# A row softmax on one core: from pooled 4-row tiles to one in-place arena with tiles of up to 16 rows and hand-placed semaphores

## The chip, the cores and the metric

The kernel runs on one core of a Trainium2 chip. The metric is the device time of one execution in microseconds (us), lower is better. Six kinds of unit matter here: the 16 DMA engines that move data between HBM and SBUF; VectorE (DVE); ScalarE (ACT), which also issues DMAs; SyncE (SP), which here only issues DMAs and waits; GpSimd (POOL), which is idle (0.2 us busy); and each engine's sequencer (ACTq, SPq). All runs compared below are fast runs of one core at clock 1.000 unless I say otherwise.

A ratio below is the mean time of one kernel's fast runs over the mean of the other kernel's fast runs of the same rounds. It is therefore not quite the ratio of the medians that I quote beside it.

## The reference

```python
# x: float32 (16, 1024, 512), so 16384 rows of 512
x_scaled = x / 2.0
x_max = np.max(x_scaled, axis=-1, keepdims=True)
exp_x = np.exp(x_scaled - x_max)
return exp_x / np.sum(exp_x, axis=-1, keepdims=True)
```

Every partition of SBUF gets 128 rows of 2 KB. 33.55 MB are read and 33.55 MB are written. Nothing is reused.

## The kernel before

A tile is 128 partitions by 4 rows (1 MB), so each partition's part of a DMA is one run of 8 KB. There are 32 tiles. Loads are issued by SP, stores by ACT, and a framework places the semaphores and may reorder the instructions of an engine.

```python
R = 4
in_pool  = ctx.enter_context(tc.tile_pool(name="inp",  bufs=8))
out_pool = ctx.enter_context(tc.tile_pool(name="outp", bufs=8))
...
def do_load(i):
    x_sb = in_pool.tile([P, R, D], fp32, name=f"x_sb")
    nc.sync.dma_start(out=x_sb, in_=xt[i])
    nc.vector.reduce_max(out=negmax, in_=x_sb, axis=mybir.AxisListType.X, negate=True)
def do_exp(i):                      # ACT, one instruction per row, plus row sums
    for r in range(R):
        nc.scalar.activation(out=e_sb[:, r], in_=x_sb[:, r], func=Exp,
            bias=negmax[:, r:r+1], scale=0.5, accum_out=sums[:, r:r+1])
    nc.vector.reciprocal(out=recip, in_=sums)
def do_mul(i):                      # DVE, one instruction per row
    ...
def do_store(i):
    nc.scalar.dma_start(out=ot[i], in_=e_sb)
for j in range(TOT):                # load j, exp j-1, multiply j-2, store j-3
    ...
```

The softmax here doesn't subtract the row's maximum and nothing guards it: scores larger than these inputs give would overflow.

Of the kernel before, what the change touches and what calls it, by code (L numbers as in the profile page):

```python
# [1 line left out]

# [4 lines left out]


@with_exitstack  # L10
def kernel(
    ctx: ExitStack,
    tc: tile.TileContext,
    x: bass.AP,
    out: bass.AP,
):
    nc = tc.nc
    fp32 = mybir.dt.float32

    xf = x.flatten_outer_dims()  # L20
    of = out.flatten_outer_dims()
    N, D = xf.shape
    P = nc.NUM_PARTITIONS

    R = 4
    rows_per_tile = P * R
    ntiles = N // rows_per_tile

    xt = xf.rearrange("(n p r) d -> n p r d", p=P, r=R)
    ot = of.rearrange("(n p r) d -> n p r d", p=P, r=R)  # L30

    in_pool = ctx.enter_context(tc.tile_pool(name="inp", bufs=8))
    out_pool = ctx.enter_context(tc.tile_pool(name="outp", bufs=8))
    st_pool = ctx.enter_context(tc.tile_pool(name="stats", bufs=8))

    LAG_EXP = 1
    LAG_MUL = 2
    LAG_ST = 3
    TOT = ntiles + LAG_ST

    x_sbs = {}
    e_sbs = {}
    negmaxs = {}
    sumss = {}
    recips = {}

    def do_load(i):
        x_sb = in_pool.tile([P, R, D], fp32, name=f"x_sb")
        nc.sync.dma_start(out=x_sb, in_=xt[i])  # L49
        negmax = st_pool.tile([P, R], fp32, name=f"negmax")  # L50
        nc.vector.reduce_max(  # L51
            out=negmax, in_=x_sb, axis=mybir.AxisListType.X, negate=True
        )
        x_sbs[i] = x_sb
        negmaxs[i] = negmax

    def do_exp(i):
        x_sb = x_sbs.pop(i)
        negmax = negmaxs[i]
        e_sb = out_pool.tile([P, R, D], fp32, name=f"e_sb")  # L60
        sums = st_pool.tile([P, R], fp32, name=f"sums")
        for r in range(R):
            nc.scalar.activation(  # L63
                out=e_sb[:, r],
                in_=x_sb[:, r],
                func=mybir.ActivationFunctionType.Exp,
                bias=negmax[:, r : r + 1],
                scale=0.5,
                accum_out=sums[:, r : r + 1],
            )  # L70
        recip = st_pool.tile([P, R], fp32, name=f"recip")
        nc.vector.reciprocal(out=recip, in_=sums)  # L72
        e_sbs[i] = e_sb
        recips[i] = recip

    def do_mul(i):
        e_sb = e_sbs[i]
        recip = recips[i]
        for r in range(R):
            nc.vector.tensor_scalar_mul(  # L80
                out=e_sb[:, r],
                in0=e_sb[:, r],
                scalar1=recip[:, r : r + 1],
            )

    def do_store(i):
        e_sb = e_sbs.pop(i)
        nc.scalar.dma_start(out=ot[i], in_=e_sb)  # L88

    for j in range(TOT):  # L90
        if j < ntiles:
            do_load(j)
        if 0 <= j - LAG_EXP < ntiles:
            do_exp(j - LAG_EXP)
        if 0 <= j - LAG_MUL < ntiles:
            do_mul(j - LAG_MUL)
        if 0 <= j - LAG_ST < ntiles:
            do_store(j - LAG_ST)


# [1 line left out]
_INS = ['x']  # L102
_OUTS = [((16, 1024, 512), 'float32')]


# [23 lines left out]
```

## Time and profile before

| | before |
|---|---|
| time | 165.8 us |
| span in the profile | 163.8 us |
| bytes moved | 67.15 MB |
| DVE busy, ACT busy | 78%, 58% |
| steady DMA rate, 24 to 136 us | 427 GB/s |

The first block holds lines of the page. The slices cut the span into 40 equal pieces, and each digit is the busy share in tenths. The GB/s row and the windows book a packet, with all of its bytes and time, where it starts, so a share can come out over 1.00. In the groups, the columns after the bar are busy time, mean ns of one instruction, and the idle time before them with its main releaser.

```profile
span 163.8 us, 663 instructions
DVE 128.3 (78%) x192; ACT 94.4 (58%) x257; POOL 0.2 (0%) x4
DVE  0599999585699689998977778978778977977540
ACT  0399777706052625776676545676555676599900
DMA  4999999999999999999999999999999999799995
GB/s 174 436 422 422 348 422 432 426 424 428 426 426 428 422 426 432 424 428 426 426 432 428 424 430 424 428 426 426 428 428 424 426 430 424 326 414 412 418 420 228
q1 hardware_dynamic: 4608, 33.56, 49.2%
q10 hardware_dynamic: 4608, 33.56, 48.7%
DMA 63%; ACT 13%; DVE 9%; issue 7%; ACTq 2%; SPq 2%; DVEq 0%
L63 ACT ACTIVATE e_sb<-x_sb,negmax 128x512 f32<-128x512 f32 x128 | 90.7, 709 | 55.6 <-DVE e_sb L80 50.5
L51 DVE TENSOR_REDUCE negmax<-x_sb 128x4 f32<-128x2048 f32 x32 | 73.0, 2282 | 24.8 <-DMA x_sb<-in_x_dram 24.8
L80 DVE TENSOR_SCALAR e_sb<-e_sb,recip 128x512 f32<-128x512 f32 x128 | 53.5, 480 | 0.9
```

The DMA row reads 9 nearly everywhere, so I take the DMA engines for the limit, and the 55.6 us of idle ACT cost nothing by themselves. Two slices stand out in the GB/s row: 348 near the start and 326 near the end. Each queue has 4608 packets: 4096 of data (32 tiles x 128 partitions, 8 KB each) and 512 semaphore writes.

The windows view puts sizes on the two dips. Its columns are the stretch, its length, busy time and count of DVE, ACT and POOL, the clock, the DMA share, and GB/s.

```profile
16.00:20.00 4.00, 4.00 (x7) 3.41 (x10) 0.00 (x0) 1.00 1.00 338
24.00:136.00 112.00, 93.46 (x131) 61.52 (x168) 0.00 (x0) 1.00 1.01 427
140.00:144.00 4.00, 3.93 (x12) 2.56 (x7) 0.00 (x0) 1.00 0.76 311
144.00:160.00 16.00, 9.74 (x27) 11.65 (x34) 0.00 (x0) 1.00 1.01 418
```

The two dips differ in kind. At 16 us the engines are fully busy (share 1.00) but slower: the load packets that start from 16 to 20 us took 395 ns on average instead of 309 from 24 to 136 us. At 140 us they are idle for a quarter of the time (share 0.76): the loads have ended and the next stores are not ready. I call that one the hole.

### The profile page before, as it was taken

What the parts mean: (1) busy time and instruction counts of PE and PEld (TensorE: products, weight loads), DVE (VectorE), ACT (ScalarE), POOL (GpSimd) and SP (SyncE); (2) the same over time, 40 slices, a digit from 0 to 9 for tenths busy, and PEclk for the clock granted to TensorE, in tenths of its full rate; (3) what the DMA queues carried; (4) which work ended last, traced back from release to release, by engine and by line L of the source; (5) the groups of instructions that cost most, each with busy time, mean ns of one, the idle gap of its engine ahead of it and who ended that gap; (6) DMA issues with size and microseconds to landing.
All of it is one profiled execution on the core that took longest, in us unless ns stands there. A gap on an engine that the chain in (4) does not pass through costs nothing.

```text
span 163.8 us, 663 instructions
## 1 busy us (share of the span) xinstructions
DVE 128.3 (78%) x192; ACT 94.4 (58%) x257; POOL 0.2 (0%) x4
## 2 busy tenths in 40 slices
DVE  0599999585699689998977778978778977977540
ACT  0399777706052625776676545676555676599900
POOL 0000000000000000000000000000000000000000
DMA  4999999999999999999999999999999999799995
GB/s 174 436 422 422 348 422 432 426 424 428 426 426 428 422 426 432 424 428 426 426 432 428 424 430 424 428 426 426 428 428 424 426 430 424 326 414 412 418 420 228
DMA packets 9221, 67.15 MB, mean 410 GB/s; under 512 B 1024, under 2 KB 1024, under 8 KB 1024
## 3 DMA queue, kind: packets, MB, share of 16 engines
q1 hardware_dynamic: 4608, 33.56, 49.2%
q10 hardware_dynamic: 4608, 33.56, 48.7%
q14 instruction: 5, 0.04, 0.1%
HBM read 33.55 MB, written 33.55 MB: 410 GB/s over the span
## 4 chain that ended last, share of the span: by engine, by line
DMA 63%; ACT 13%; DVE 9%; issue 7%; ACTq 2%; SPq 2%; DVEq 0%
DMA x_sb<-in_x_dram 63%; ACT e_sb L63 13%; DVE e_sb L80 6%; DVE negmax L51 3%; ACTq L88 2%; SPq L49 2%; DVE recip L72 1%; DVEq L124 0%; ACTq L63 0%
## 5 line engine op out<-in xcount | busy, mean ns | idle before, releaser
L63 ACT ACTIVATE e_sb<-x_sb,negmax 128x512 f32<-128x512 f32 x128 | 90.7, 709 | 55.6 <-DVE e_sb L80 50.5
L51 DVE TENSOR_REDUCE negmax<-x_sb 128x4 f32<-128x2048 f32 x32 | 73.0, 2282 | 24.8 <-DMA x_sb<-in_x_dram 24.8
L80 DVE TENSOR_SCALAR e_sb<-e_sb,recip 128x512 f32<-128x512 f32 x128 | 53.5, 480 | 0.9
L63 ACT ACTIVATION_READ_ACCUMULATOR e_sb<-x_sb,negmax 128x1 f32 x128 | 23.9, 187 | 0.0
L72 DVE RECIPROCAL recip<-sums 128x4 f32<-128x4 f32 x32 | 5.4, 169 | 3.7 <-ACT e_sb L63 3.7
L63 ACT ACT_TABLE_LOAD x1 | 1.3, 1283 | 5.6 <-DMA x_sb<-in_x_dram 5.6
L113 POOL MEMSET const-uint8-127<- 128x1 uint8 x1 | 0.1, 102 | 0.0
L113 POOL MEMSET const-bfloat16-1.0<- 128x1 bf16 x1 | 0.1, 101 | 0.0
L113 POOL MEMSET const-float32-0.0<- 128x1 f32 x1 | 0.1, 99 | 0.2 <-issue 0.2
L113 POOL MEMSET const-float32-1.0<- 128x1 f32 x1 | 0.1, 98 | 0.0
## 6 DMA issues: line engine op xcount, KB each, us to landing
x_sb<-in_x_dram SPq DMA_DIRECT2D x32, 1024.0 KB, 12.2
out_dram<-e_sb ACTq DMA_DIRECT2D x32, 1024.0 KB, 10.0
```

Source lines behind the costliest of these rows:

```text
L49: nc.sync.dma_start(out=x_sb, in_=xt[i])
L51: nc.vector.reduce_max(out=negmax, in_=x_sb, axis=mybir.AxisListType.X, negate=True)
L63: nc.scalar.activation(out=e_sb[:, r], in_=x_sb[:, r], func=mybir.ActivationFunctionType.Exp, bias=negmax[:, r : r + 1], scale=0.5, accum_ ...
L72: nc.vector.reciprocal(out=recip, in_=sums)
L80: nc.vector.tensor_scalar_mul(out=e_sb[:, r], in0=e_sb[:, r], scalar1=recip[:, r : r + 1],)
L88: nc.scalar.dma_start(out=ot[i], in_=e_sb)
L113: nc = _bacc.Bacc("TRN2", target_bir_lowering=False, num_devices=1)
```

## The change

The intent is to keep DMA busy from end to end. One tensor ("arena") of 100 rows per partition holds everything and each row is computed in place. Tiles grow to 16 rows, so a partition's run is up to 32 KB. Eight loads (100 rows) are issued at once on ACT's queue. The last 28 rows reuse the places of early tiles, and their loads are issued on SP between the stores. All waits are placed by hand.

```diff
+PLAN = [                      # (rows, place in the arena)
+    (4, 0), (8, 4), (16, 12), (16, 28), (16, 44), (16, 60), (16, 76),
+    (8, 92), (16, 12), (8, 4), (4, 0),
+]
+ARENA = 100
+CHUNK = 4
+LAG = 2
...
-    R = 4
-    in_pool = ctx.enter_context(tc.tile_pool(name="inp", bufs=8))
-    out_pool = ctx.enter_context(tc.tile_pool(name="outp", bufs=8))
+    arena = nc.alloc_sbuf_tensor("arena", (P, ARENA, D), fp32)
...
+    def dram(ap, t):
+        b, r, _ = tiles[t]
+        return ap[b * P : (b + r) * P].rearrange("(p r) d -> p r d", r=r)
...
+    with tc.tile_critical():
+        for t in range(len(tiles)):
+            if t not in behind:          # behind: tiles whose place it reuses
+                nc.scalar.dma_start(out=sb(t), in_=dram(xf, t)).then_inc(ld[t], 16)
+        for k, (t, b, a) in enumerate(chunks):
+            ...  # ACT: exp of 4 rows in place, waits s_max, then s_exp
+        for k in range(len(chunks) + LAG):
+            ...  # DVE: max of chunk k (waits ld), multiply of chunk k-2 (waits s_exp)
+        late = sorted(behind)
+        for t in range(len(tiles)):
+            nc.sync.wait_ge(s_mul, last_chunk[t] + 1)
+            nc.sync.dma_start(out=dram(of, t), in_=sb(t)).then_inc(st[t], 16)
+            while late and max(behind[late[0]]) <= t - 2:
+                u = late.pop(0)
+                for v in behind[u]:
+                    nc.sync.wait_ge(st[v], 16)
+                nc.sync.dma_start(out=sb(u), in_=dram(xf, u)).then_inc(ld[u], 16)
+        for t in range(len(tiles)):
+            nc.sync.wait_ge(st[t], 16)
```

## The prediction

> **What bounds the kernel now.** The DMA engines: the page's slices show them 90% or more busy from slice 2 to the end; DVE is 78% busy, ACT 58%. The windows view gives a steady 427 to 428 GB/s (24 to 136 us), at which 67.15 MB take 157 us of the 163.8 us span. The other 6 to 7 us, from the windows view: 2.4 us before bytes flow, 0.8 us in a dip to 311-319 GB/s at 17 to 20 us when stores begin, 1.1 us at 140 to 142 us (DMA share 0.70 and 0.39: loads have ended, stores are not ready), 0.5 us because the stores-only end runs at about 418 GB/s, and 1.7 us after the last bytes. The large idle sums in the waits view (ACT 55.6 us, DVE 24.8 us) cost nothing by themselves.

> **What the change does.** Bytes and compute stay the same (reduction 2.29 us per 4 rows, exp 0.71 us and multiply 0.42 us a row, reciprocal 0.17 us). In one arena, 100 of 128 rows per partition are requested at once; the last 28 reuse early rows.

> 1. The 140 us hole closes. DVE needs about 4.2 us per 4-row chunk. I estimate that it waits for the third tile until about 21 us, then runs without a break to about 147 us. Loads end near 120 to 125 us with two tiles or more of finished stores queued; the last stores become ready about 137, 145 and 147 us, ahead of the DMA. Gain 1.1 us, all critical.
> 2. Fewer, longer descriptors: 22 DMAs in place of 64, runs of 32 KB for 96 of 128 rows in place of 8 KB. Fewer semaphore writes (9 ns each, 64 down to 22 per engine): 0.4 us. At the steady rate an 8 KB packet costs about 305.5 ns[...]. [...]
> 3. Swapping queues does nothing to bandwidth; it frees ACT of 0.34 us per store, off the critical path. Late loads travel on SP's queue before the stores of tile 5; they do not starve the DMA.
> 4. Against it: the stores-only end grows from about 20 to 37 us at 2% less bandwidth, minus 0.4 us. Start-up and tail are unchanged.

> **Sum.** 165.8 - 1.1 - 0.4 - 0.7 + 0.4 - 0.7 (a softer dip) = 163.3 us. Range 161.6 to 165.0. Faster by over 2%: 0.30; within 2%: 0.66; slower by over 2%: 0.04.

> **What would show it.** Right: no slice below 90% DMA between slice 2 and the last; no hole near 140 us; steady rate 428 to 433 GB/s; DVE almost continuously busy from about 21 to 147 us and done over 8 us before the end; a chain of waits dominated by DMA. The packet count shows whether long runs stay whole (about 2,800 data packets in place of 8,192). Wrong: a hole before the last stores, DVE stalled on loads after 21 us, or 8 KB packets as before.

> **What would make it wrong.** [...] long packets slowing one direction or leaving engines uneven at the end; stores held behind the late loads so that DMA idles; a slower start with ACT issuing.

The sum came to 163.3 us. The first "- 0.7" in it is half of an estimate for the longer runs that rested on figures no trace or run shows. Without it the sum would be 164.0 us. Two more things rest on such figures: the upper end of the steady rate, 433 GB/s, and a case under what would make it wrong.

## The result and the profile after

The changed kernel takes 164.37 us (median of four fast runs, 163.9 to 164.8) against 165.76 us. The ratio is 0.9912, with a 95% interval of 0.989 to 0.9933. A second set on another occasion gave 164.5 us and 0.9916. The change gains 0.9%, which is within 2%.

These are the answering lines of the page after:

```profile
span 162.7 us, 528 instructions
DVE 127.0 (78%) x192; ACT 95.0 (58%) x257; POOL 0.2 (0%) x4
DVE  0539199999999999999976999997999999920000
ACT  0378547777777777777770777775777777600000
DMA  4999998989999999999999999999999999999992
GB/s 161 427 443 508 395 419 379 486 371 411 447 449 395 475 427 403 475 411 395 443 451 419 407 435 425 443 435 387 389 457 435 419 451 389 435 483 403 411 413 103
q1 hardware_dynamic: 2016, 40.90, 59.0%
q10 hardware_dynamic: 1152, 26.21, 38.1%
DVE 53%; DMA 33%; issue 1%; ACTq 1%; SPq 0%
L99 DVE TENSOR_REDUCE negmax<-arena 128x4 f32<-128x2048 f32 x32 | 72.9, 2280 | 15.3 <-DMA arena<-in_x_dram 15.3
```

The computing is the same and from 20 us on it runs with two short breaks; it ends at 143.4 us, and the last four DVE slices are 0. The queues hold 2016 + 1152 = 3168 packets: 2816 of data and 352 semaphore writes, so the 32 KB runs travel whole. The GB/s row scatters more mostly because a long packet is booked into the slice where it starts: spread over their durations, the packets give 430 GB/s and a share of 1.00 for 16 to 20 us, where the windows view below says 508 and 1.21. In the chain, DVE has replaced DMA as the largest share. That looks like a new limit, and experiment 3 tests it.

The same windows after:

```profile
16.00:20.00 4.00, 0.89 (x3) 2.68 (x8) 0.00 (x0) 1.00 1.21 508
24.00:136.00 112.00, 107.49 (x165) 79.71 (x219) 0.00 (x0) 1.00 1.01 428
140.00:144.00 4.00, 3.39 (x9) 1.01 (x4) 0.00 (x0) 1.00 1.13 483
144.00:160.00 16.00, 0.00 (x0) 0.00 (x0) 0.00 (x0) 1.00 0.93 400
```

The hole at 140 us is gone. The steady rate is 428 GB/s against 427. The last line is low because packets that started before 144 us are booked earlier and because most engines have finished before 160 us. Spread over their durations, the packets run at 432 GB/s from 144 to 158 us, against 418 in the kernel before.

The trace records every packet with its start and duration. For each DMA it holds 16 semaphore writes (352 for 22 DMAs, 1024 for 64); I take those of the last store for one from each engine when its part has landed. From these I made a ledger. "Bulk ends" is the median of those 16 last writes.

| us | before | after | difference |
|---|---|---|---|
| bulk of the engines ends at | 161.91 | 159.59 | -2.32 |
| the last engine after the bulk | 0.69 | 1.36 | +0.67 |
| last semaphore to the end of the span | 1.16 | 1.71 | +0.55 |
| span | 163.75 | 162.67 | -1.09 |

Within the -2.32 us: the first byte comes at 1.92 instead of 1.75 us (+0.17), the hole had cost 0.99 us per engine (-0.99), packets above their usual duration (the median for their size) took 2.14 us per engine more than usual instead of 1.68 (+0.46), and the rest, about -2.0 us, I put down to the longer packets and the fewer semaphore writes. Their usual durations in the trace are 309 ns (8 KB), 611 ns (16 KB) and 1213 ns (32 KB). Where a single engine is left alone in a trace (the tail of experiment 9), the starts of its packets follow each other every 306 ns and 607 ns, so a packet costs about 301 ns per 8 KB plus 5 ns each. For the plan of the changed kernel that is 96 x 1209 + 48 x 607 + 32 x 306 ns = 155.0 us per engine, where the 1209 ns are extrapolated, against 512 x 306 ns = 156.7 us before: 1.7 us less. Forty-two fewer semaphore writes per engine add an estimated 0.2 us, at about 5 ns each: their records take 9 ns, of which I take off the 3 to 4 ns by which a packet overlaps the next (309 against 306 ns, 611 against 607).

So the gain was there, about 2.3 us, and half of it was given back in the last three microseconds. These are single executions; the second traced execution of the changed kernel (experiment 11) has nearly the same end.

### The profile page after: what moved, and what is told of

Read it like the earlier page. It is cut to its first block, busy times and chain, and to the rows that moved or that the text cites. A ratio compares the mean times of both kernels' runs of the same rounds, so it can differ in the third digit from the quotient of the medians.

```text
span 162.7 us, 528 instructions
## 1 busy us (share of the span) xinstructions
DVE 127.0 (78%) x192; ACT 95.0 (58%) x257; POOL 0.2 (0%) x4
## 3 DMA queue, kind: packets, MB, share of 16 engines
q1 hardware_dynamic: 2016, 40.90, 59.0%
q10 hardware_dynamic: 1152, 26.21, 38.1%
## 4 chain that ended last, share of the span: by engine, by line
DVE 53%; DMA 33%; issue 1%; ACTq 1%; SPq 0%
DMA arena<-in_x_dram 33%; DVE negmax L99 28%; DVE arena L112 24%; DVE recip L108 1%; ACTq L81 1%; SPq L131 0%; ACTq L164 0%; SPq L70 0%
## 5 line engine op out<-in xcount | busy, mean ns | idle before, releaser
L84 ACT ACTIVATE arena<-arena,negmax 128x512 f32<-128x512 f32 x128 | 90.8, 710 | 40.9 <-DVE negmax L99 40.9
L99 DVE TENSOR_REDUCE negmax<-arena 128x4 f32<-128x2048 f32 x32 | 72.9, 2280 | 15.3 <-DMA arena<-in_x_dram 15.3
L112 DVE TENSOR_SCALAR arena<-arena,recip 128x512 f32<-128x512 f32 x128 | 53.6, 482 | 1.1
L84 ACT ACTIVATION_READ_ACCUMULATOR arena<-arena,negmax 128x1 f32 x128 | 23.9, 187 | 0.0
```

Source lines behind the costliest of these rows:

```text
L84: ins = nc.scalar.activation(out=arena[:, a + r], in_=arena[:, a + r], func=mybir.ActivationFunctionType.Exp, bias=negmax[:, b + r : b + r ...
L99: nc.vector.reduce_max(out=negmax[:, b : b + CHUNK], in_=arena[:, a : a + CHUNK], axis=mybir.AxisListType.X, negate=True,)._wait_ge(ld[t], ...
L112: ins = nc.vector.tensor_scalar_mul(out=arena[:, a + r], in0=arena[:, a + r], scalar1=recip[:, b + r : b + r + 1],)
```

## The experiments

My theory was: DMA limits both kernels; longer runs and the closed hole bring about 3 us; the loss is at the end, from engines that finish late and from the exit of the critical section. The rivals were that DVE is the new limit (the chain), that the number of DMAs or the freer buffers rather than the run length give the gain, and that computing beside the DMAs slows them.

### 1. The same kernel with 8 KB runs

```diff
-        return ap[b * P : (b + r) * P].rearrange("(p r) d -> p r d", r=r)
+        return ap[b * P : (b + r) * P].rearrange("(c p r) d -> p c r d", p=P, r=CHUNK)
-        return arena[:, at : at + r, :]
+        return arena[:, at : at + r, :].rearrange("p (c r) d -> p c r d", r=CHUNK)
```

> The changed kernel with the same 22 DMAs, arena, queues and semaphores, but each tile's DRAM rows cut into blocks so that every contiguous run is 8 KB again. If the length of the descriptors pays (32 KB packets took 1213 ns, 8 KB ones 309 ns, about 2.4 to 3 ns of which overlap the next packet), the time rises by about 1.8 us to 166.2 us and the packet count to 8,192. If the number of DMAs or the order of work pays instead, it stays within 0.4 us of 164.4 us. Also: if long packets are what spreads the ends of the 16 engines (1.9 us in the changed kernel, 0.8 us before), the spread shrinks to under 1 us here.

It took 175.89 us, ratio 1.0616 (1.0602 to 1.063). The time missed both expectations: the loss is 11.5 us where I expected 1.8. (The last engines did end close together, 0.08 us after the bulk, but experiment 7 shows that this does not come from the short runs.) The reason is in ACT's stream. These are the lines for ACT's eight load instructions (duration in ns: minimum, median, maximum; then first and last start in us), first of the changed kernel:

```profile
L81 ACTq DMA_DIRECT2D arena<-in_x_dram x8: 376/466/767, 0.9 to 4.6; - x8
```

and of the short-run version, followed by its line of the waits view:

```profile
L81 ACTq DMA_DIRECT2D arena<-in_x_dram x8: 393/2387/9599, 0.9 to 26.3; - x8
```

```profile
ACT L84 <- issue: 35.9, 1, 35.9
```

```profile
92.00:100.00 8.00, 7.93 (x13) 5.87 (x16) 0.00 (x0) 1.00 0.26 104
```

All in all, issuing its eight loads took ACT 35.0 us here, against 4.2 us in the changed kernel.

### 2. The kernel before with 6 input and 18 output buffers

```diff
-    in_pool = ctx.enter_context(tc.tile_pool(name="inp", bufs=8))
-    out_pool = ctx.enter_context(tc.tile_pool(name="outp", bufs=8))
+    in_pool = ctx.enter_context(tc.tile_pool(name="inp", bufs=6))
+    out_pool = ctx.enter_context(tc.tile_pool(name="outp", bufs=18))
```

> The kernel before with 6 input and 18 output buffers in place of 8 and 8 (192 KB a partition, no arena, 8 KB runs). If the hole at 140 us came from computing that had to wait for output buffers, it closes and the time falls by about 1.0 us to 164.8 us. The rival says that the hole is the plain end latency of load, compute and store: then it stays and the time is within 0.3 us of 165.8 us.

It took 165.83 us, ratio 1.0012 (0.9996 to 1.0028): no gain. The windows show that the hole only moved, and shrank from 0.99 to 0.59 us per engine in the packet records:

```profile
140.00:144.00 4.00, 3.12 (x5) 2.93 (x8) 0.00 (x0) 1.00 1.02 428
144.00:148.00 4.00, 3.93 (x12) 2.13 (x6) 0.00 (x0) 1.00 0.87 360
```

More output buffers are not what closes it, at least not at the price of two input buffers, which the same edit took away. In the kernel before, DVE at 130 us has done the maxima of 120 rows but the multiplies of 89; at 140 us it is 128 and 97. DVE's stream waits for new loads (24.8 us in all) while rows that are already exponentiated wait behind them. The changed kernel keeps the two 8 to 12 rows apart. With 18 output buffers they are 22 rows apart at 130 us instead of 31, and the hole is smaller, which fits. That this order is the cause is argued, not tested alone.

### 3. The changed kernel with half of the reduction

```diff
-                in_=arena[:, a : a + CHUNK],
+                in_=arena[:, a : a + CHUNK, : D // 2],
```

> The changed kernel with the reduction over 256 of 512 columns (softmax does not depend on the shift, so the result stays right): about 35 us less DVE work. The chain of waits gives DVE 53% of the span; if DVE is the limit the time falls by many us. If the DMA engines are the limit, as I hold, it stays within 0.5 us of 164.4 us.

The result stays correct. It took 163.79 us, ratio 0.9889 (0.9875 to 0.9903). These are its busy time and its chain by engine:

```profile
DVE 93.2 (58%) x192; ACT 94.7 (58%) x257; POOL 0.2 (0%) x4
DMA 51%; DVE 26%; another core or an unknown queue 5%; ACTq 1%; issue 0%; SPq 0%
```

DVE lost 34 us of work and the kernel gained 0.6 us by the medians (0.4 us by the ratios). DVE is not the limit. The chain misled, because it starts from the last computing instruction and not from the last store. In the changed kernel that is the last multiply, and this is the last piece of its chain:

```profile
141.75 1.67 DVE arena L112 x4
```

So the chain ends at 143.4 us and leaves the last 19 us out (its shares add up to 88%). The last store was issued at 143.5 us and its packets then stood 13 to 17 us in a queue behind other stores. Where DMAs end the kernel, look at where the chain ends, and at how long the last DMA was queued, before you believe the chain.

### 4 and 5. The DMAs alone, with long and with short runs

Both are the changed kernel without exp and DVE; a tile is stored as it was loaded, so the result is wrong.

```diff
-        for k, (t, b, a) in enumerate(chunks):      # all of ACT's and DVE's work
-            ...
-            nc.sync.wait_ge(s_mul, last_chunk[t] + 1)
+            nc.sync.wait_ge(ld[t], 16)
```

The second has the edit of experiment 1 as well.

> The changed kernel's DMAs alone: no exp, no DVE, each tile is stored as it was loaded (a wrong result on purpose). It measures the floor that the DMA side sets by itself. If DMA is the limit: 163 to 164.5 us, no more than 1 us below the changed kernel. If compute costs more than that, it is clearly faster.

> The copy alone (no exp, no DVE, wrong on purpose) with 8 KB runs in place of 16 and 32 KB. Beside the copy with long runs (162.56 us) this is the length of the descriptors alone: the packets of the traces (1213 ns for 32 KB, 4 x 309 ns, minus an overlap of 2.4 to 2.8 ns each) say plus 1.8 us, 164.4 us. If the length has another cost while DMAs stay queued (the short-run version of the whole kernel lost 11.5 us), it is several us slower than that, up to 174 us.

Long runs: 162.56 us, ratio 0.981 (0.9797 to 0.9824). Short runs: 164.72 us, ratio 0.9927 (0.9915 to 0.994). The difference of the ratios, 0.0117 of 165.8 us, is 1.9 us, give or take 0.3 by the two intervals, and this is the length of the runs alone: both copies have 22 DMAs and the same 352 semaphore writes. It agrees with the 1.7 us from the packet durations; the traced copies also differ by 0.4 us in packets above the usual duration (1.23 and 1.64 us per engine). The 0.2 us for fewer semaphore writes is not tested here. In my prediction I had taken 0.7 us for the length of the runs, half of an estimate that was not shown by any trace. The first copy came out slightly below the range I had given for it (1.8 us below the changed kernel, where I had said at most 1 us), so computing does cost something; experiment 6 asks what.

The 5 ns for each packet, taken from the 306 and 607 ns between starts, are 1.6% of an 8 KB packet.

### 6. Few instructions

```diff
-            for r in range(CHUNK):
-                ins = nc.scalar.activation(... bias=..., accum_out=...)
+            nc.scalar.activation(out=arena[:, a : a + CHUNK], in_=arena[:, a : a + CHUNK],
+                func=mybir.ActivationFunctionType.Exp, scale=0.5)
-            for r in range(CHUNK):
-                ins = nc.vector.tensor_scalar_mul(...)
+            nc.vector.tensor_scalar_mul(out=arena[:, a : a + CHUNK], in0=arena[:, a : a + CHUNK],
+                scalar1=recip[:, b : b + 1])
```

The reduction is over 256 columns here as well.

> The changed kernel with one ACT and three DVE instructions per 4-row chunk in place of 8 and 6 (no shift, one scale for 4 rows: a wrong result on purpose), DMAs and semaphores as they were. Theory: the last engines finish 0.4 to 1.4 us after the others because they also carry the instruction fetches (8 KB packets of the instruction queue, 309 ns each, 4 in the changed kernel, none in the copy). Then the instruction queue moves nothing here, the ends of the 16 engines lie within 0.6 us, and the time is about 162.9 us. Rival: it is computing beside the DMAs, or slow packets, that spread them: then the spread stays over 1 us and the time is 163.7 us or more.

It took 163.1 us, ratio 0.9831 (0.9817 to 0.9844). One fetch packet was left. The last engine ended 0.41 us after the bulk, and all 16 within 0.78 us, a little more than the 0.6 us I had expected. By the ratios this is 0.35 us over the copy, where the changed kernel is 1.7 us over it. Most of what separates the changed kernel from the copy therefore goes when instructions and work are taken away together. DVE's work is also smaller here, but experiment 3 had shown that this alone brings 0.4 us and leaves the last engine 1.49 us late. ACT's work is smaller too (62.3 us busy instead of 95.0), and this was not tested alone; experiment 9 adds instructions only.

Part of the difference is slow packets. From 24 to 136 us their excess per engine is 0.00 us in the long copy, 0.39 with half of the reduction, 0.46 here, 0.56 in the raw version (experiment 8) and 1.48 and 1.22 in the two traces of the changed kernel. The raw version computes as much as the changed kernel, so neither the long packets nor the computing beside them gives a fixed excess.

### 7. Short runs, loads issued between the exps

```diff
+        after_chunk = {0: 4, 2: 5, 5: 6, 7: 7}
-        for t in range(len(tiles)):
-            if t not in behind:
-                nc.scalar.dma_start(...)
+        for t in range(4):
+            load(t)
...
             ins.then_inc(s_exp, 1)
+            if k in after_chunk:
+                load(after_chunk[k])
```

The edit of experiment 1 is in it too.

> The whole kernel with 8 KB runs as in the first experiment, but the last four of ACT's eight loads issued between its exp instructions, so that the queue never holds more than about 50 rows. Theory: the 11.5 us were lost because ACT stood 35 us in its first eight DMA instructions [...], and the exps stood behind them. Then ACT starts at about 8 us and the time is about 166.2 us, the changed kernel plus 1.8 us for the packets. If short runs cost more for another reason, it stays over 170 us.

It took 165.55 us, ratio 0.9978 (0.9965 to 0.999). Of the 11.5 us about ten are back, so ACT's blocking in its first eight loads was the cause. (Two of the four moved loads still blocked ACT, for 1.4 and 4.7 us.) What is left against the changed kernel is 0.9978 - 0.9912 = 0.0066, 1.1 us. That is less than the 1.9 us of the copies; most of the difference is that the packets above their usual duration cost 1.52 us here and 2.14 us in the changed kernel.

So the long runs do two things in this design. They save about 1.9 us, and with them ACT issues its eight loads in 4.2 us instead of 35.0.

### 8. The changed kernel without the framework's context

```diff
-    with _tile.TileContext(nc) as tc:
-        tile_softmax_temp_2p0_kernel(tc, *args)
+    tc = _Raw(nc)       # nc, nc.alloc_semaphore, and a null context for tile_critical
+    tile_softmax_temp_2p0_kernel(tc, *args)
```

> The changed kernel's instructions without the framework's context around them (no entry and exit of the critical section). The changed kernel ends 1.7 us after its last semaphore write, the kernel before 1.2 us. If the exit chain is the difference, this one ends 0.6 to 1.0 us after it and the time is 0.5 to 0.8 us below the changed kernel, about 163.7 us. If not, it is the same as the changed kernel, 164.4 us.

The result is correct. It took 162.46 us (161.55 to 163.1), ratio 0.9805 (0.9785 to 0.9825). It beats both kernels, by more than I expected. First the page's span line and then, for the line of the final waits on the stores, SP's semaphore instructions of the raw version:

```profile
span 160.2 us, 493 instructions
```

```profile
L138 SPq EVENT_SEMAPHORE  x6: 17/28/28, 143.0 to 160.2; - x6
```

and the same kind of line of the changed kernel, with one of the lines of the framework's exit after it, and that line of the kernel before:

```profile
L138 SPq EVENT_SEMAPHORE  x5: 27/28/28, 143.8 to 161.3; - x5
L164 POOLq EVENT_SEMAPHORE  x4: 17/17/17, 161.9 to 162.6; - x4
L124 POOLq EVENT_SEMAPHORE  x4: 17/17/17, 163.1 to 163.6; - x4
```

In the changed kernel SP's last such wait starts at 161.3 us and the exit goes on to 162.6 us. In the raw version that wait is the end: 0.43 us after the last semaphore write, against 1.71 us. ACT's first load is also issued at 0.72 instead of 0.90 us. Together that is 1.46 us, and it is the whole context, not the critical section alone: the kernel before has the framework's exit too and ends 1.16 us after its last semaphore write. What the critical section adds is the 0.55 us of the ledger. The trace has instructions for it: those of line 70, which opens the section, run from 161.35 to 161.75 us, before the framework's exit.

The traced raw execution was the fastest of its five (161.55 us), and its span is 2.46 us shorter than that of the changed kernel. The other 1.0 us is a last engine that was 1.00 instead of 1.36 us late and a bulk that ended another 0.63 us earlier, 0.38 us of it in slow packets. That these come from the missing context is not shown.

### 9. Only instructions added

This is experiment 6 with 1,024 tiny writes on the idle GpSimd.

```diff
+        scratch = nc.alloc_sbuf_tensor("scratch", (P, 1024), fp32)
+        for n in range(1024):
+            nc.gpsimd.memset(scratch[:, n : n + 1], 0.0)
```

> The few-instructions kernel (163.1 us, wrong on purpose) plus 1,024 tiny writes on the idle GpSimd into a scratch tensor nobody reads. It adds only instruction fetches: about 8 more packets of 8 KB on the instruction queue, 309 ns each. If fetches are what makes one or two DMA engines finish late, and they all sit on one or two engines, the last semaphore comes 1.2 to 2.5 us after the bulk and the time rises to 164.3 to 165.6 us. If they are spread over the engines or cost nothing, it stays within 0.4 us of 163.1 us and the late engines of the changed kernel have another cause.

The fast runs took 167.66 to 169.74 us, ratio 1.018 (1.0135 to 1.0225), 3.5% above experiment 6 and more than I expected. The traced execution (171.5 us) was counted as slow, being over 1.5% above the fastest of its kind, at clock 1.000. In it, by the semaphore writes, 15 engines had finished their part of the last store by 159.38 us. One was still at the third last store then, and wrote the semaphores of the last three stores at 160.62, 165.48 and 167.93 us. With 1,024 instructions added on an engine that computes nothing of use, one DMA engine was 9.2 us late (0.41 us in experiment 6), long after they had ended: the last of the writes starts at 44.3 us. Whether it is the instructions as such or the writes into SBUF that they do was not separated, so the "only" of my expectation is not shown.

The recorded instruction fetches explain only part. There are nine packets of 8 KB, 2.8 us if all fell on that engine, and it is 9.2 us late. The records carry no engine number, so I could not follow the late engine with certainty through the crowded part of the trace; from 159.4 us on, alone, it runs without gaps and at the usual durations. What else made that engine late is open.

The traces of all runs, in this respect:

| kernel | instructions | DMA idle late in the run | last engine after the bulk, us |
|---|---|---|---|
| copy, long runs (4) | 77 | no | 0.30 |
| copy, short runs (5) | 77 | no | 0.19 |
| few instructions (6) | 208 | no | 0.41 |
| raw (8) | 493 | no | 1.00 |
| changed kernel, twice | 528 | no | 1.36, 1.59 |
| half reduction (3) | 528 | no | 1.49 |
| short runs, spread (7) | 528 | no | 1.63 |
| few + 1,024 (9) | 1235 | no | 9.19 |
| before | 663 | the hole at 141 us | 0.69 |
| 18 output buffers (2) | 655 | the hole at 145 us | 0.72 |
| short runs (1) | 528 | at 153 us | 0.08 |
| queues swapped (10) | 644 | from 170 us on | 0.10 |

I read the table so: an engine that has fallen behind catches up when the others must wait. The kernel before had such a pause 20 us before its end. The changed kernel, having closed the hole, has none, so its lateness piles up to the end. Where no pause came, the last engine is later the more instructions there are. This reading fits all thirteen traces, but the pause was never added or removed by itself.

### 10. The kernel before with only the queues swapped

```diff
-        nc.sync.dma_start(out=x_sb, in_=xt[i])
+        nc.scalar.dma_start(out=x_sb, in_=xt[i])
-        nc.scalar.dma_start(out=ot[i], in_=e_sb)
+        nc.sync.dma_start(out=ot[i], in_=e_sb)
```

> The kernel before with one part of the change alone: loads issued by ACT, stores by SP, pools and framework kept. My prediction held that the swap does nothing. But the framework then orders ACT's stream as three loads, then one load after every four exps, so loads are at most three or four 1 MB tiles ahead in place of eight. Theory now: DMA starves at the start (loads at the pace of computing) and the time rises, about 168 us (166.5 to 171). If the swap is free, or frees ACT of waiting for stores and closes the hole at 140 us, it is 164.8 to 165.8 us.

The fast runs took 181.55 to 184.24 us, ratio 1.1037 (1.099 to 1.1084). The direction was right and the size was not: 17 us lost by the ratio where I expected 2. The edit also changes when loads are issued: in the trace, ACT issues three loads and then one after every four or five exps. The window of the steady part and the longest wait of DVE (the traced execution was a slow one at 185.8 us, clock 1.000):

```profile
24.00:136.00 112.00, 80.47 (x121) 58.27 (x161) 0.00 (x0) 1.00 0.99 382
DVE negmax L51 <- DMA x_sb<-in_x_dram: 47.4, 29, 5.6
```

The DMA share is 0.99 and yet the rate is 382 GB/s. The load packets took 366 ns on average instead of their usual 309 (a tenth of them over 531 ns), while the stores stayed at 310. Above their usual duration, packets took 15.0 us per engine against 1.7 in the kernel before, two thirds of the 20 us by which the two traces differ; a start without loads, which I had expected, is the smaller part. At the start of a reduction only one further load had been issued, against seven at first, falling to two, in the kernel before. Here a busy share of 0.99 did not mean full speed: compare the packets' durations. Why the load packets take longer is open. It is not the short queue alone: in the kernel before there are times with as few load packets waiting (under 12 per engine, as almost always here; 1,072 packets between 24 and 136 us), and they took 309 ns.

The changed kernel has the same swap without this loss. Its loads are issued far ahead, by the arena and the hand-placed order; that this is what makes the swap free was not tested alone. In the changed kernel, DVE's waits for loads sum to 15.3 us, of which 11.8 us lie in the first 20 us.

### 11. The changed kernel once more

> The changed kernel once more, to have its ratio and its slow packets in the same round as others: 164.4 us, ratio 0.991, last engines 0.8 us or more after the bulk, and about 1.7 us from the last semaphore write to the end. If the ratio is 0.985 or below, the comparison of the raw version with it (0.9805) was a matter of the chip's state.

164.5 us, ratio 0.9916 (0.9895 to 0.9937), the last engine 1.59 us after the bulk, 1.73 us from there to the end, and 2.32 us of slow packets. The gap to the raw version is not a matter of the occasion.

## Why the prediction was right or wrong

The time was inside the range, 1.1 us above the middle, and "within 2%" was right. The gain was 1.4 us and not the predicted 2.5 us. Some of this is luck: by the ledger, start and end cost 1.4 us that the sum did not have, and slow packets cost 0.5 us where the sum had counted on 0.7 us less. Of these 2.6 us, 1.3 us were hidden because long runs gave 0.9 us more than predicted and the 0.4 us of step 4 were not lost. Step by step:

- **What bounds the kernel:** right. For the changed kernel experiments 3 and 4 show it; for the kernel before it is read from the slices and from the steady rate.
- **Step 1, the hole closes, 1.1 us:** right, 0.99 us. DVE ran from 20.3 to 143.4 us, near my 21 to 147. It did wait for late loads twice after 21 us (2.6 us at 84 us and 0.95 us at 111 us), one of the signs I had named for being wrong. It cost nothing, because stores were queued.
- **Step 2, longer runs, 0.7 + 0.4 us:** the direction was right and the size too small. The copies give 1.9 us for the length of the runs; the fewer semaphore writes, at 5 ns and not 9, give about 0.2 us by the trace. The 0.7 us were half of an estimate that no trace showed. I also missed the second effect: with 8 KB runs this order of issue blocks ACT for 35.0 us and loses 11.5 us (experiment 1).
- **Step 3, the swap does nothing:** true of the whole change, wrong as a general statement. Alone, with the framework's order of loads, it costs 10% (experiment 10).
- **Step 4, 0.4 us lost in a longer stores-only end:** wrong. From 124 us to the end, the changed kernel's stores had next to no packet above the usual duration (0.03 us per engine; 0.43 for all packets of the kernel before), and from 144 to 158 us they ran at 432 GB/s against 418.
- **"A softer dip", 0.7 us:** wrong. The dip at 16 to 20 us went, but slow packets came at other times (28 to 36, 96 to 100 and 116 to 120 us in the profiled run), and their sum grew by 0.46 us. Those between 24 and 136 us sum to about 1.5 us per engine (0.1 in the kernel before) and so cancel the gain of the long packets in that window, hence 428 against 427 GB/s. Their cause is open.
- **"Start-up and tail are unchanged":** this is the step that failed. The start cost 0.17 us, the late engines 0.67 us and the exit of the critical section 0.55 us. Together 1.4 us were given back. The prediction had named uneven engines and a slower start among the things that would make it wrong, but gave them no time. Long packets are not what makes the engines uneven: with 8 KB runs the last one is 1.63 us late (experiment 7).
- **"A chain dominated by DMA":** wrong. The chain said DVE 53%, and the chain was the misleading view. "No slice below 90%" also fails on the page, where two slices read 8; spread over their durations, the packets give every slice from the second to the last but one 0.99 or more.

## What to carry to other kernels

In this kernel, with DMA busy nearly from end to end (a share of 1.01 at 427 GB/s), the remaining gain was in the bytes per descriptor (8 KB to mostly 32 KB: 1.9 us of 166) and in the first and last three microseconds, so write down what happens after the last byte: leaving out the framework's exit saved 1.3 us, about as much as the whole change had gained, though the kernel before paid 0.7 us of it too. Before you put a long list of loads on an engine that also computes, count the packets that it leaves in flight, because here ACT stood 35.0 us in its own loads, with an estimated 92 to 108 packets per engine outstanding. Do not take the chain of waits for the limit when it ends long before the kernel does and queued DMAs fill the rest (here it ended 19 us early and gave DVE 53%); take work away from the accused engine and see (34 us less of DVE brought 0.4 us).
